# Norm scales spread over the partitions through a row in DRAM instead of by products with the identity

## The chip, the core and the metric

The program runs on one core of one Trainium2 chip. The metric is the device time of one execution in microseconds (us), the median over several. The core's engines work side by side, each through its own queue in order: TensorE (PE) multiplies matrices into PSUM, VectorE (DVE) and ScalarE (ACT) work on tiles, GpSimd (POOL) here does small powers, and SyncE (SP) issues the transfers (DMAs). Semaphores let one engine wait for another.

## The reference

Two layers of a decoder trunk over 512 tokens of width 1024, in float32. Per layer:

```
hn   = rms_norm(h, g_mix);  proj = hn @ w_in          # q | k | v | xr | gr
o    = rms_norm(diff_attention(rope(q), rope(k), v), g_subln) * (1 - lam_init)   # 4 heads
y    = rg_lru(conv(xr)) * gelu(gr)
h    = h + concat(o, y) @ w_out
h    = h + square(relu(rms_norm(h, g_mlp) @ w_mlp_in)) @ w_mlp_out
gate = sigmoid(rms_norm(h, g_ple) @ w_ple_gate)
h    = h + gate * (p[l] @ w_ple_proj)                 # the PLE step
out  = rms_norm(h, g_final)                           # after the last layer
```

Each rms_norm multiplies every token by one number, 1 / sqrt(mean square + eps).

## The kernel before

Activations lie transposed: a tile h[m] holds 128 features on the partitions and the 512 tokens along the free dimension. A product is done in three passes over split operands (high and low parts in a rounded float32 format), which `mm3` issues; a projection of 128 outputs is 8 x 3 = 24 products `dense` of 128x512. Weights come in chunks of 128x1024 (`raw`), and ACT and DVE split each into `wh` and `wl`.

A norm isn't applied to the input of a projection but to its output, since one number per token commutes with the product. `Norm.stats` sums squares over the partitions by four small products (`msq`) that leave the sums with the tokens on the partitions, 128x4; DVE adds eps (`me`), and POOL takes the power -0.5 (`rT`; for the MLP norm DVE takes the reciprocal, since the squared ReLU squares the factor, too). What multiplies a 128x512 output needs these 512 numbers along the free dimension and the same on all partitions. That is the job of `spread`. Before, it issues four products in which the identity is the moving operand and a column of r, broadcast to 128 columns, the stationary one. They are float32 and appear as two records each, eight per spread, under the name `bc`. For a norm ACT copies the result to SBUF (`rbc`); for a head of attention DVE multiplies from PSUM.

There are seven spreads per layer: the first norm (users: the multiplies `xp` behind the recurrent branch's projections, and more later), one for each of the four heads in `head_out` (sums `osm`, scales `orT`, multiply `o<-o`, then split into `oh` and `ol` for the output projection), the MLP norm (users: `dn` behind the down projection) and the PLE norm (users: `gt` behind the gate projection). The final norm, `FinalNorm`, has its own products of the name `bc`, which the change leaves.

The order of the work isn't the order of the code. `Plan` records every operation, and `Plan.schedule` lists them by a model: each engine has a clock, each operation a cost, the oldest ready operation of the engine that is free first is issued, and tiles come from pools of fixed size. A DMA is modelled as 1.15 us, then its bytes at 355 GB/s in one line with all other DMAs, then 0.9 us. `Plan.add` finds what an operation depends on by its tiles. Every operation therefore appears on one line of the profile, L182, and is told apart by its tiles.

PSUM holds six banks for projections and scores (tag `pm`) and two for small results (`ps`), among them `bc`. In the PLE step `ple` takes two banks for the `pj` products and two for the gates per pair of outputs, so the second pair's gates need banks that the first pair gives back.

Of the kernel before, what the change touches and what calls it, by code (L numbers as in the profile page):

```python
# [11 lines left out]
F32 = mybir.dt.float32  # L12
F32R = mybir.dt.float32r
I32 = mybir.dt.int32
AF = mybir.ActivationFunctionType
ALU = mybir.AluOpType
AX = mybir.AxisListType

S = 512
NT = S // 128  # L20
# [45 lines left out]
class Plan:  # L66
# [73 lines left out]
    def add(self, eng, fn, method, args, kw):  # L140
        i = len(self.nodes)
        outs = [a for a in list(args[:1]) + [kw.get("out"), kw.get("accum_out")] if hasattr(a, "free_size")]
        ins = [a for a in list(args[1:]) + [v for k, v in kw.items() if k not in ("out", "accum_out")]
               if hasattr(a, "free_size")]
        deps, uses = set(), set()
        for aps, write in ((ins, False), (outs, True)):
            for a in aps:
                if a.space == bass.MemoryType.DRAM:
                    continue
                t = self.tiles.get(a.name)  # L150
                if t is None:
                    t = self.tiles[a.name] = {"w": [], "r": [], "n": 0, "first": i,
                                              "tag": self.tags[self.index[a.name]] if a.name in self.index else None}
                deps.update(t["w"])
                if write:
                    deps.update(t["r"])
                uses.add(a.name)
        for a in ins:
            if a.name in self.tiles:
                self.tiles[a.name]["r"].append(i)  # L160
        for a in outs:
            t = self.tiles.get(a.name)
            if t is not None:
                t["w"], t["r"] = ([i], []) if t["r"] or eng == "pe" else (t["w"] + [i], [])
        for u in uses:
            self.tiles[u]["n"] += 1
        deps.discard(i)
        size = 0
        if "dma" in method:
            size = kw["out"].nbytes if not callable(kw["out"].nbytes) else kw["out"].nbytes()  # L170
        func = kw.get("func")
        self.nodes.append(dict(eng=eng, fn=fn, args=args, kw=kw, deps=deps, uses=uses, cost=self.cost(eng, method, args, kw),
                               pri=i - self.boost, size=size, set=self.SETS.get(func, 0)))
        if eng == "pe":
            out = args[0]
            rows = (kw["lhsT"] if "lhsT" in kw else args[1]).partition_size()
            self.nodes[-1]["cols"] = out.free_size() * rows / 128 * (1 if kw.get("rhs", out).dtype == F32R else 4 if "rhs" in kw else 2)
# [223 lines left out]
def build(ctx: ExitStack, tc: tile.TileContext, given, x, p, pos, w, vec, lamqk, out):  # L401
    rnc = tc.nc
    nc = Plan(rnc, WIN, ('raw', 'wh', 'wl'), given)
    act = nc.scalar.activation
    ve = nc.vector
    mm = nc.tensor.matmul
# [5 lines left out]
    wsp = ctx.enter_context(tc.tile_pool(name="ws", bufs=1))  # L412
    psm = ctx.enter_context(tc.tile_pool(name="psm", bufs=1, space=bass.MemoryType.PSUM))
    pss = ctx.enter_context(tc.tile_pool(name="pss", bufs=1, space=bass.MemoryType.PSUM))

    def T(name, dt=F32, n=S):
        return nc.tile(tp, [128, n], dt, "t", TB, name)
# [4 lines left out]
    def PS(name):  # L422
        return nc.tile(pss, [128, S], F32, "ps", 2, name)
# [71 lines left out]
    def take(kind, l, *rest):  # L495
        i = cur[0]
        assert CHUNKS[i] == (kind, l, *rest), (CHUNKS[i], kind, l, rest)
        w_split(i)
        cur[0] += 1
        return w_t.pop(i)  # L500
# [5 lines left out]
    def split(src, hi, lo):  # L506

        act(out=hi, in_=src, func=AF.Copy)
        ve.tensor_tensor(out=lo, in0=src, in1=hi.bitcast(F32), op=ALU.subtract)
# [11 lines left out]
    ident = const.tile([128, 128], F32, name="ident")  # L521
# [146 lines left out]
    class Norm:  # L668
# [33 lines left out]

        def spread(self):
            self.bc = T("rbc")
            spread(self.rT, 0, self.bc)

    def spread(r, c, dst):
        ps = PS("bc")
        for j in range(NT):
            mm(ps[:, j * 128:(j + 1) * 128], lhsT=r[:, c + j:c + j + 1].to_broadcast([128, 128]), rhs=ident,  # L710
               start=True, stop=True)
        if dst is None:
            return ps
        act(out=dst, in_=ps, func=AF.Copy)

    class FinalNorm:

# [57 lines left out]
    def layer(l, h, nm, last):  # L775
# [107 lines left out]
        for j in range(NT):  # L883
            hi, lo = T("vh", F32R), T("vl", F32R)
            r = nm.rT[:, j:j + 1]
# [115 lines left out]

        def head_out(hd):
            o, r = ho.pop(hd)
            ps = spread(r, 0, None)
            ve.tensor_tensor(out=o, in0=o, in1=ps, op=ALU.mult)
            hi, lo = T("oh", F32R), T("ol", F32R)
            split(o, hi, lo)
            yo[hd] = (hi, lo)

        def push_head(hd, q, k):  # L1010
            for qi in range(NT):
                unit_scores(hd, qi, q, k)
                unit_max(hd, qi)
                unit_mix(hd, qi)
                unit_T(hd, qi)
            head_av(hd)
            head_norm(hd)
            head_out(hd)
# [55 lines left out]
        for g in (ORDER[0:3], ORDER[3:6], ORDER[6:8]):  # L1074
            ws = []
            for m in g:
                c = take("out", l, m)
# [15 lines left out]
        for q in range(NQ):  # L1093
# [57 lines left out]
            for i0 in range(0, KD, 2):  # L1151
                ws = []
                for m in ORDER[i0:i0 + 2]:
                    c = take("down", l, m, q)
# [111 lines left out]
def trunk(tc, x, p, pos, w, vec, lamqk, out):  # L1266
    import concourse.bacc as bacc
    nc = bacc.Bacc("TRN2", target_bir_lowering=False, num_devices=1)
    a = [nc.dram_tensor(f"a{i}", t.shape, t.dtype, kind="ExternalInput").ap() for i, t in enumerate((x, p, pos, w, vec, lamqk, out))]
    with tile.TileContext(nc) as t0:  # L1270
        plan = build(t0, None, *a)
    build(tc, plan, x, p, pos, w, vec, lamqk, out)
# [64 lines left out]
```

## Time and profile before

| | us |
|---|---|
| median of 3 runs | 1205.5 (1205.45 to 1206.63) |
| profiled execution, its time | 1205.26 |
| its span | 1203.1 |
| PE busy | 1185.9 (99%), 6784 matmuls |
| DVE busy | 946.3 (79%) |
| ACT busy | 665.8 (55%) |
| POOL busy | 21.6 (2%) |

The span runs from the first to the last instruction of the program; the time holds 2.2 us more. A busy time is the union of an engine's records; PE's records overlap, so that the distance from one start to the next tells what a product costs, and not its record's length. The chain of waits follows the work that ended last back through what released it. Stretches in the trace are named by microseconds from the span's start: layer 0 has its attention from about 40 to 172 us, its MLP up to 547, its PLE step up to 592; layer 1 follows in the same way, with attention up to 761 and the PLE step from 1132 on.

### The profile page before, as it was taken

What the parts mean: (1) busy time and instruction counts of PE and PEld (TensorE: products, weight loads), DVE (VectorE), ACT (ScalarE), POOL (GpSimd) and SP (SyncE); (2) the same over time, 40 slices, a digit from 0 to 9 for tenths busy, and PEclk for the clock granted to TensorE, in tenths of its full rate; (3) what the DMA queues carried; (4) which work ended last, traced back from release to release, by engine and by line L of the source; (5) the groups of instructions that cost most, each with busy time, mean ns of one, the idle gap of its engine ahead of it and who ended that gap; (6) DMA issues with size and microseconds to landing.
All of it is one profiled execution on the core that took longest, in us unless ns stands there. A gap on an engine that the chain in (4) does not pass through costs nothing.

```text
span 1203.1 us, 17586 instructions
## 1 busy us (share of the span) xinstructions
PE 1185.9 (99%) x6784; PEld 1040.7 (87%) x6784; DVE 946.3 (79%) x1704; ACT 665.8 (55%) x1084; POOL 21.6 (2%) x44
## 2 busy tenths in 40 slices
PE   8999999999999999999999999999999999999996
PEld 6877788988988989988888888899899898898896
DVE  8899989987787678575778999898786787776564
ACT  6878747743643535543458787476355254364352
POOL 1000010000000000000000000000000000000000
PEclk9999999999999999999999999999999999999998
DMA  6321132243323333332323202324332333342202
GB/s 238 105 71 51 38 123 88 89 141 103 108 92 100 107 97 114 106 106 88 94 71 103 83 2 77 116 89 133 95 106 89 105 106 105 93 127 97 88 1 71
DMA packets 34371, 114.70 MB, mean 95 GB/s; under 512 B 3952, under 2 KB 6000, under 8 KB 34288
## 3 DMA queue, kind: packets, MB, share of 16 engines
q1 hardware_dynamic: 34288, 113.59, 30.0%
q8 instruction: 53, 0.87, 0.3%
q14 instruction: 30, 0.25, 0.1%
HBM read 111.48 MB, written 2.10 MB: 94 GB/s over the span
## 4 chain that ended last, share of the span: by engine, by line
PE 88%; DVE 6%; ACT 3%; DMA 1%; issue 1%; POOL 0%; SPq 0%; POOLq 0%; DVEq 0%; ACTq 0%
PE dense L182 53%; PE up L182 27%; PE pv L182 2%; PE pj L182 2%; PE bc L182 1%; DVE pr L182 1%; PE av L182 1%; DVE qr L182 1%; PE sc L182 1%; ACT ky L182 1%; DVE wl L182 1%; DVE q L182 1%; PE msq L182 1%; ACT pr L182 1%; POOL orT L182 0%
## 5 line engine op out<-in xcount | busy, mean ns | idle before, releaser
L182 ACT ACTIVATE wh<-raw 128x1024 fp32r<-128x1024 f32 x204 | 214.3, 1057 | 280.1 <-PE dense L182 150.3
L182 DVE TENSOR_TENSOR wl<-raw,wh 128x1024 fp32r<-128x1024 f32 x204 | 248.0, 1220 | 22.2 <-ACT wh L182 21.8
L182 PE MATMUL dense<-ffh,wh 128*128 128x512 f32 x512 | 199.5, 390 | 0.0
L182 PE MATMUL dense<-ffh,wl 128*128 128x512 f32 x512 | 199.3, 389 | 0.0
L182 PE MATMUL dense<-ffl,wh 128*128 128x512 f32 x512 | 199.3, 389 | 0.0
L182 PE MATMUL dense<-hgh,wl 128*128 128x512 f32 (+1 forms) x400 | 150.5, 376 | 1.4 <-DVE wl L182 1.2
L182 PE MATMUL dense<-hgl,wh 128*128 128x512 f32 (+1 forms) x400 | 150.9, 377 | 0.0
L182 PE MATMUL dense<-hgh,wh 128*128 128x512 f32 (+1 forms) x400 | 150.5, 376 | 0.1
L182 PEld LDWEIGHTS dense<-ffh,wl 128*128 128x128 f32 x512 | 96.1, 188 | 20.2
L182 PEld LDWEIGHTS dense<-ffh,wh 128*128 128x128 f32 x512 | 96.2, 188 | 19.6
L182 PEld LDWEIGHTS dense<-ffl,wh 128*128 128x128 f32 x512 | 96.2, 188 | 19.5
L182 DVE TENSOR_TENSOR dn<-dense,rbc 128x512 f32<-128x512 f32 x64 | 44.2, 691 | 73.4 <-PE dense L182 72.5
L182 PE MATMUL up<-bh,wl 128*128 128x256 f32 x352 | 99.6, 283 | 0.0
L182 PE MATMUL up<-bl,wh 128*128 128x256 f32 x352 | 99.6, 283 | 0.0
L182 PE MATMUL up<-bh,wh 128*128 128x256 f32 x352 | 99.5, 283 | 0.0
L182 ACT ACTIVATE sh<-s 128x512 fp32r<-128x512 f32 x96 | 60.0, 628 | 70.9 <-DVE s L182 70.2
L182 PEld LDWEIGHTS dense<-hgh,wl 128*128 128x128 f32 x400 | 75.5, 189 | 13.6 <-DVE wl L182 1.9
L182 PEld LDWEIGHTS dense<-hgh,wh 128*128 128x128 f32 x400 | 75.5, 189 | 12.2 <-DVE q L182 0.4
L182 PEld LDWEIGHTS dense<-hgl,wh 128*128 128x128 f32 x400 | 75.5, 189 | 12.0
L182 PE MATMUL up<-bh,sl 128*128 128x256 f32 x288 | 81.5, 283 | 0.0
L182 PE MATMUL up<-bl,sh 128*128 128x256 f32 x288 | 81.5, 283 | 0.0
L182 PE MATMUL up<-bh,sh 128*128 128x256 f32 x288 | 81.3, 283 | 0.0
(235 smaller groups left out, 2549.6 us busy)
## 6 DMA issues: line engine op xcount, KB each, us to landing
raw<-w SPq DMA_DIRECT2D x204, 512.0 KB, 3.6
h<-x SPq DMA_DIRECT2D x8, 256.0 KB, 5.3
out<-fin SPq DMA_DIRECT2D x8, 256.0 KB, 2.2
w<-w SPq DMA_DIRECT2D x4, 256.0 KB, 4.3
pT<-p SPq DMA_DIRECT2D x4, 256.0 KB, 3.3
lq<-lamqk SPq DMA_DIRECT2D x1, 256.0 KB, 7.1
vt<-vec SPq DMA_DIRECT2D x1, 61.0 KB, 2.2
posi<-pos SPq DMA_DIRECT2D x1, 2.0 KB, 2.9
```

The source lines that it names most:

```text
L182: d["fn"](*d["args"], **d["kw"])
```

## The change

`spread` no longer multiplies. It takes a tile of 4x128 in DRAM, writes the 128x4 scales into it token by token, and reads it back to all 128 partitions at once, both through POOL's DMA queue. The result lies in SBUF in each case, so a head gets a tile `obc`, and the ACT copy for the norms goes. `Plan.add` now follows tiles in DRAM as well, so the read waits for the write.

```
-                if a.space == bass.MemoryType.DRAM:
+                if a.space == bass.MemoryType.DRAM and a.name not in self.index:
...
+    drp = ctx.enter_context(tc.tile_pool(name="dr", bufs=1, space=bass.MemoryType.DRAM))
...
-            spread(self.rT, 0, self.bc)
-
-    def spread(r, c, dst):
-        ps = PS("bc")
-        for j in range(NT):
-            mm(ps[:, j * 128:(j + 1) * 128], lhsT=r[:, c + j:c + j + 1].to_broadcast([128, 128]), rhs=ident,
-               start=True, stop=True)
-        if dst is None:
-            return ps
-        act(out=dst, in_=ps, func=AF.Copy)
+            spread(self.rT, self.bc)
+
+    def spread(r, dst):
+
+        row = nc.tile(drp, [NT, 128], F32, "row", 4, "row")
+        nc.gpsimd.dma_start(out=row.rearrange("j p -> p j"), in_=r, allow_slow_non_contiguous=True)
+        nc.gpsimd.dma_start(out=dst, in_=row.rearrange("j p -> (j p)").unsqueeze(0).to_broadcast([128, S]))
...
-            ps = spread(r, 0, None)
-            ve.tensor_tensor(out=o, in0=o, in1=ps, op=ALU.mult)
+            bc = T("obc")
+            spread(r, bc)
+            ve.tensor_tensor(out=o, in0=o, in1=bc, op=ALU.mult)
```

The planner makes a new order from this. On PE, in the PLE step of layer 0, behind the statistics and the last six products of the first two gates:

```order
 L182 MATMUL pj<-pTh,wh 128x512
 L182 MATMUL pj<-pTl,wh 128x512
-L182 MATMUL bc<-ident,rT 128x128 x4
 L182 MATMUL pj<-pTh,wl 128x512
 L182 MATMUL pj<-pTh,wh 128x512
```

The group bc is taken out, and nothing else moves there: the twelve pj products stand where they stood, and behind them the gates of the second pair.

On DVE, at the first head of layer 0, from the mean square `ome` of the head's output to the multiply of that output; before:

```order
L182 SCALAR_TENSOR_TENSOR ome<-ome,osm 128x4
L182 TENSOR_TENSOR wl<-raw,wh 128x1024
L182 TENSOR_TENSOR kl<-q_398,ky 64x512
L182 TENSOR_TENSOR at<-tr,at 128x128
L182 TENSOR_TENSOR kl<-q_398,ky 64x512
L182 RECIPROCAL s_358<-s_358 128x1
L182 TENSOR_SCALAR mx<-mx 128x2
L182 TENSOR_TENSOR o<-o,bc 128x512
```

And now on DVE the last of the rows ahead of the same multiply, with the first behind it:

```order
L182 TENSOR_TENSOR at<-tr,at 128x128
L182 ISA pr,mx<-sc,mask 128x512
L182 ISA mx 128x1
L182 RECIPROCAL s_361<-s_361 128x1
L182 TENSOR_TENSOR wl<-raw,wh 128x1024
L182 SCALAR_TENSOR_TENSOR s_361<-s_361,nlam,s_352 128x1
L182 RECIPROCAL s_368<-s_368 128x1
L182 TENSOR_SCALAR mx<-mx 128x2
L182 SCALAR_TENSOR_TENSOR pr<-pr,s_361 128x256
L182 TENSOR_TENSOR wl<-raw,wh 128x1024
L182 TENSOR_TENSOR o<-o,obc 128x512
L182 TENSOR_TENSOR at<-tr,at 128x2x128
```

Twenty instructions stand between the two now, where six stood: softmax work of later blocks of the same head and a second weight split have moved ahead of the multiply.

## Rows read from the trace of the kernel before

**Rows 1.** The page: engines' busy time, and the weight queue (packets, MB, share).
```profile
PE 1185.9 (99%) x6784; PEld 1040.7 (87%) x6784; DVE 946.3 (79%) x1704; ACT 665.8 (55%) x1084; POOL 21.6 (2%) x44
...
q1 hardware_dynamic: 34288, 113.59, 30.0%
```

**Rows 2.** The chain of waits in order of time: start, duration, what.
```profile
20.23 0.79 PE msq L182 x8
...
30.74 1.16 PE bc L182 x8
...
167.93 0.80 PE osm L182 x8
...
168.99 1.93 POOL orT L182
...
251.91 0.89 PE bc L182 x8
...
503.03 43.55 PE dense L182 x192
```

**Rows 3.** Windows of both attention stages: length, PE, PEld, DVE, ACT, POOL busy, PE clock, DMA.
```profile
40.00:172.00 132.00, 127.49 (x633) 103.84 (x632) 125.47 (x299) 101.56 (x192) 6.84 (x4) 1.00 0.22 69
616.00:761.00 145.00, 144.64 (x717) 120.72 (x716) 131.96 (x298) 107.30 (x197) 5.23 (x4) 1.00 0.24 77
```

**Rows 4.** Timeline at the PLE norm of layer 0: start, duration, engine, operation.
```profile
559.46 0.49 PE L182 MATMUL dense<-hgh,wh 128*128 128x512 f32 x1
...
559.88 1.01 POOL L182 TENSOR_TENSOR rT<-me,mhalf 128x4 f32<-128x4 f32 x1 [388.97 <-DVE me L182]
...
561.41 1.05 PE L182 MATMUL bc<-ident,rT 128*128 128x128 f32 x8
...
562.22 0.47 PE L182 MATMUL pj<-pTh,wl 128*128 128x512 f32 x1
...
563.63 1.28 DVE L182 TENSOR_TENSOR gt<-dense,rbc 128x512 f32<-128x512 f32 x2
...
564.60 0.40 PE L182 MATMUL dense<-hgh,wh 128*128 128x512 f32 x1
```

**Rows 5.** Who waited for whom: us in total, times, longest.
```profile
PEld bc L182 <- POOL orT L182: 2.3, 4, 0.7
```

**Rows 6.** Groups by form, 100 to 172 us: busy, mean ns, idle before.
```profile
L182 DVE TENSOR_TENSOR wl<-raw,wh 128x1024 fp32r<-128x1024 f32 x11 | 13.4, 1217 | 0.0
...
L182 DVE CUSTOM_DVE_ANT_0 pr<-sc,mask 128x512 f32<-128x512 f32 x6 | 4.1, 686 | 0.0
...
L182 DVE TENSOR_TENSOR o<-o,bc 128x512 f32<-128x512 f32 x3 | 2.1, 687 | 0.9 <-PE bc L182 0.9
...
L182 ACT ACTIVATE oh<-o 128x512 fp32r<-128x512 f32 x3 | 1.9, 627 | 0.9 <-DVE o L182 0.9
```

**Rows 7.** DMA issues: times, KB each, median us from issue to landing.
```profile
out<-fin SPq DMA_DIRECT2D x8, 256.0 KB, 2.2
...
pT<-p SPq DMA_DIRECT2D x4, 256.0 KB, 3.3
lq<-lamqk SPq DMA_DIRECT2D x1, 256.0 KB, 7.1
vt<-vec SPq DMA_DIRECT2D x1, 61.0 KB, 2.2
posi<-pos SPq DMA_DIRECT2D x1, 2.0 KB, 2.9
```

**Rows 8.** The heads' scales on POOL: ns min/median/max.
```profile
L182 POOL TENSOR_TENSOR orT<-ome,mhalf x8: 1006/1455/1989, 110.8 to 757.1; 128x4 f32<-128x4 f32 x8
```

**Rows 9.** Windows around PE's waits at the start and end, columns as in rows 3.
```profile
8.00:12.00 4.00, 3.57 (x9) 2.32 (x10) 3.59 (x6) 4.00 (x8) 0.00 (x0) 0.59 1.02 376
...
1192.00:1196.00 4.00, 1.65 (x7) 1.57 (x8) 0.80 (x3) 0.81 (x2) 0.69 (x1) 0.65 0.00 0
1196.00:1200.00 4.00, 1.01 (x4) 0.72 (x4) 2.48 (x4) 0.00 (x0) 0.00 (x0) 0.50 0.34 113
```

## The prediction

> **What bounds the kernel now.** First the page: TensorE (PE) is busy for 1185.9 of 1203.1 us [rows 1], so look at the chain of waits: it is PE from end to end outside the attention stages, and a product of the form dense takes 43.55 / 192 = 0.227 us [rows 2]. Then the windows of the two attention stages: VectorE (DVE) is busy for 125.47 of 132 us in layer 0 and for 131.96 of 145 us in layer 1 [rows 3]. So there PE and DVE are both nearly full, and time lost on either ends up in the span; elsewhere only PE counts. POOL and the DMA queues are nearly idle: q1 takes 30.0% of the DMA engines [rows 1].
>
> **What goes.** Fourteen spreads (per layer one for the first norm, four heads, the MLP norm, the PLE norm) lose four float32 products with the identity each, eight records on PE. In the chain such a group stands at 0.89 to 1.16 us [rows 2]; at the PLE norm the next product starts 0.81 us after it [rows 4]. I take 0.9: 14 x 0.9 = 12.6 us off PE, all of it on the path outside attention (ends 11.3 and 16.2 by 0.81 and 1.16). PE's own wait for POOL ahead of these products goes too, 2.3 us [rows 5]. The six copies of the product on ScalarE (ACT) go from an engine that is busy for 55% [rows 1]: nothing. The multiply of a head reads the scales from SBUF instead of PSUM, 0.69 us as before [rows 6]: nothing.
>
> **What comes.** Each spread becomes two DMAs on POOL's queue, the second behind the first's landing, and the multiply on DVE behind the second. POOL has only the next power behind them, and SP's queue of weight loads isn't passed. What counts is D, the time from r (the 128x4 scales) to the landed 128x512 tile. No transfer before is issued by POOL, goes out in 4-byte pieces, or goes through DRAM, so D is bounded from landings [rows 7]. Low: two of the shortest, vt and out, 2.2 + 2.2 = 4.4 us. High: the row is 512 pieces, 32 per engine; a packet took 0.300 x 16 x 1203.1 / 34288 = 0.168 us of an engine [rows 1], so 2.2 + 32 x 0.168 = 7.6; the read back has the shape of lq, 7.1 us beside the opening loads; together 14.7. Nearest rows: posi moves 128 pieces of 16 bytes in 2.9, 0.7 above vt; four times as many pieces, 2.2 + 4 x 0.7 = 5.0; pT brings 256 KB in 3.3. I take D = 5.0 + 3.3 = 8.3 us.
>
> The Trainium skill, "DMA: Bandwidth & Descriptors", section "Anatomy of one DMA — SWDGE (gpsimd) path", gives a POOL-issued DMA about 2.0 us plus its bytes at 436 GB/s, which would make D an estimated 4.6 us; the 2.2 us of out is the row here nearest to that, but from SP's queue. The same page, section "Rules for kernel authors", says that a strided last dimension becomes one descriptor per element and advises against it, which speaks against the row write; no run so far shows its price.
>
> **PLE norm, twice.** r is ready at 559.88 + 1.01 = 560.89, PE is past the statistics at 559.46 and has 6 + 12 products until it needs a PSUM bank that the first gate multiply gives back (the order shows the same 18 with bc taken out): 559.46 + 18 x 0.227 = 563.5. The bank is free at 560.89 + 8.3 + 0.7 = 569.9. PE waits 6.4 us; before it went on without a wait [rows 4]. Behind that multiply on DVE stand the second gate and all of h. Two layers: 12.8 us.
>
> **Heads 0 to 2 of each layer.** The planner has put DVE work under its guess of the transfers: in the new order 20 instructions stand between ome and o of the first head, before 6. By the durations of their forms (two weight splits wl at 1.22, two masked maxima pr at 0.69, and 16 shorter ones of 0.69 down to 0.08; [rows 6] has the first two) they sum to 8.3 us. The power takes 1.0 to 2.0 us [rows 8], 1.7 with its handoffs, and D follows: DVE waits 1.7 + 8.3 - 8.3 = 1.7 us; the other heads have 7.4 to 8.5 us of such work, so I take 2.0. Behind o on DVE stand pr and at, for which the transposes wait, and DVE has 5% to 9% of slack. Six heads: 12 us.
>
> **Last head of each layer.** 45 products follow its osm before the output projection needs oh. PE is there at 168.73 + 45 x 0.227 = 178.9. Oh is there at 170.92 + 8.3 + 0.69 + 0.63 = 180.5 [rows 2, 6]. 1.6 us; in layer 1, with a power of 1.0, 0.7. Together 2.3.
>
> **Layer starts.** In layer 0 r comes at 30.7, where bc started. PE passes msq at 21.0 and has 73 products, until 37.6, before the third V group needs the bank of the first xr group, free at 30.7 + 8.3 + 0.8 = 39.8 [rows 2]: 2.2 us. In layer 1 there are 63 products, then the gates of the recurrence, which need three multiplies and a convolution first: nothing to 1 us, I take 0.7.
>
> **MLP norm, twice.** r is made in the up projection, and the first product that depends on the spread stands 133 and 155 instructions later, some 30 us of PE. Nothing, even at D = 14.7.
>
> **Clock.** Behind the last gates, where PE was busy for 1.65 of 4 us, the granted clock fell to 0.65 and then 0.50, which is 1.2 GHz; after the opening waits it was 0.59 over 4 us [rows 9]. Two waits of 6.4 us should do this too: 4 x 0.41 = 1.6 us each, 3.3.
>
> **Sum.** -12.6 - 2.3 + 12.8 + 12 + 2.3 + 2.9 + 3.3 = +18.4 us. The profiled execution took 1205.26 us, 2.2 above its span and within 0.3 of the median 1205.5: 1205.3 + 18.4 = 1223.7, say **1224 us**. Around it each us of D counts at 12 places. At the low end, D = 4.4, only PLE still waits, 2 x 2.5: 1205.3 - 14.9 + 5.0 = 1195.4. At 14.7: 1224 + 6.4 x 12 = 1301.
>
> **Rivals.**
> A, the transfers land like the shortest rows. With D of 4.4 to 6 the DVE work covers them and only PLE waits, 5.0 to 8.2 us against 14.9 gained: 1195 to 1199 us, faster. For it: out, a write to DRAM, lands in 2.2. Against: that is from SP in long pieces, and posi's short ones were slower. The page's 2.0 us and bytes would give this case, an estimated 1196. The sides change at about D = 6.8, where PLE costs 2 x 4.9, the heads about 3 and the clock 2 to 3.
>
> B, the 4-byte pieces go one after another. With D of 11 or more all twelve waits are longer by at least 2.7: 1256 us and up, slower. For it: a packet's mean 0.168 us. Against: those are mostly 4 KB packets, and a small one should be shorter. The page's rule of one descriptor per element points here.
>
> C, the removal is hidden anyway in attention. Eight of the 14 groups stand in stretches where DVE is busy for 95% and 91% [rows 3], so their 7.2 us come off an engine that would wait for DVE: 1231 us, slower. For it: those shares. Against: PE too is busy for 127.5 of 132 and 144.6 of 145 there.
>
> **How the numbers follow.** The forecast (D of 7 to 10, 1208 to 1244 us) gets 0.42, A 0.27, B 0.18, C 0.13. Under 0.2% (2.4 us) this kernel's time can't be told from no change; A's upper edge (0.02) and the forecast's lower one (0.05) make 0.07 the same, the rest of A 0.25 faster, and 0.37 + 0.18 + 0.13 = 0.68 slower. The range of 1196 to 1262 leaves out A's lowest part (0.05) and most of B (0.13). The forecast's own range is 1208 to 1244.
>
> **What would show it.** In the profile of the changed kernel: row and rbc landings that sum to 7 to 10 us from r; at PLE, DVE gt waiting on a DMA and PE standing still for 5 to 8 us, twice, with a granted clock under 1 behind it; DVE o waiting on a DMA about 2 us in six heads; no wait at dn; PE's products of bc down to those of the final norm. It is wrong if the two landings sum to under 6.8 us (then faster), if PE's idle time is not at these places, or if time is lost in the MLP stages, where I expect none.

## The result, and the profile after

The changed kernel takes 1337.1 us (1333.0 to 1337.7, median of 4 runs) where the kernel before takes 1206.1 on the same chip: 1.108 times as long, with an interval of 1.106 to 1.110, or 131 us more. The prediction said 1224, in a range of 1196 to 1262: the direction was right, the size was not.

The page of the changed kernel's profile, against [rows 1]:

```profile
span 1335.0 us, 17406 instructions
...
PE 1209.6 (91%) x6672; PEld 1051.4 (79%) x6672; DVE 947.2 (71%) x1704; ACT 664.3 (50%) x1078; POOL 38.5 (3%) x72
```

The work is nearly the same. PE has lost 112 records, 14 groups of 8; its share of the span fell from 99% to 91%. So the 132 us are waiting, and products at a lower clock. The DMA issues of the changed kernel, where the last column is the median time from issue to landing, against [rows 7]:

```profile
raw<-w SPq DMA_DIRECT2D x204, 512.0 KB, 3.6
...
obc<-row POOLq DMA_DIRECT2D x8, 256.0 KB, 4.1
...
rbc<-row POOLq DMA_DIRECT2D x6, 256.0 KB, 4.5
...
row<-orT POOLq DMA_DIRECT2D x8, 2.0 KB, 9.3
row<-rT POOLq DMA_DIRECT2D x6, 2.0 KB, 9.5
```

Writing 2 KB takes over twice as long as reading 256 KB back. With 0.3 us from the power to the write's issue and 0.6 from its landing to the issue of the read, D, the time from the scales to the landed tile, is 0.3 + 9.3 + 0.6 + 4.1 = 14.3 us for a head and 0.3 + 9.5 + 0.6 + 4.5 = 14.9 for a norm; the prediction took 8.3. The timeline of the changed kernel at the PLE norm of layer 0, against [rows 4] (start, duration, engine, operation, in brackets the idle time before it and what ended that):

```profile
611.70 1.04 POOL L182 TENSOR_TENSOR rT<-me,mhalf 128x4 f32<-128x4 f32 x1 [292.75 <-DVE me L182]
...
613.03 0.81 POOL L182 DMA_DIRECT2D row<-rT  x1 [0.29 <-POOL rT L182]
...
615.27 0.39 PE L182 MATMUL pj<-pTh,wl 128*128 128x512 f32 x1
...
623.10 0.56 POOL L182 DMA_DIRECT2D rbc<-row  x1 [9.26 <-DMA row<-rT]
629.77 1.29 DVE L182 TENSOR_TENSOR gt<-dense,rbc 128x512 f32<-128x512 f32 x2 [11.98 <-DMA rbc<-row]
...
630.51 0.79 PE L182 MATMUL dense<-hgh,wh 128*128 128x512 f32 x1 [14.85 <-DVE gt L182]
...
631.10 0.63 PE L182 MATMUL dense<-hgl,wh 128*128 128x512 f32 x1
```

PE issues the last pj product at 615.27 and the next gate at 630.51: it stands still for 15.0 us beyond one product. Here D runs from the end of the power, 611.70 + 1.04 = 612.74, to the start of the multiply: 629.77 - 612.74 = 17.0 us, the longest of the fourteen. The place and the chain (row, read, multiply, PSUM bank, PE) are those of the prediction.

The windows of this stretch (length, PE, PEld, DVE, ACT, POOL busy, granted clock, DMA share, GB/s), against [rows 9]:

```profile
612.00:616.00 4.00, 3.66 (x16) 2.65 (x15) 2.36 (x2) 2.54 (x3) 1.54 (x2) 1.00 1.08 28
616.00:620.00 4.00, 0.00 (x0) 0.00 (x0) 1.23 (x1) 0.53 (x1) 0.00 (x0) 0.89 0.51 25
620.00:624.00 4.00, 0.00 (x0) 0.00 (x0) 0.00 (x0) 0.00 (x0) 0.56 (x1) 0.50 0.76 27
624.00:628.00 4.00, 0.00 (x0) 0.00 (x0) 0.00 (x0) 0.00 (x0) 0.00 (x0) 0.50 0.85 334
...
632.00:636.00 4.00, 4.00 (x11) 3.12 (x10) 3.43 (x6) 2.38 (x4) 0.00 (x0) 0.50 0.02 4
636.00:640.00 4.00, 4.00 (x18) 3.24 (x18) 1.18 (x3) 1.26 (x2) 0.00 (x0) 0.97 0.00 0
```

Two things are to be seen. Behind the wait the granted clock is 0.50, which is 1.2 GHz, for some 6 us of work: 11 products in 4 us where 18 fit. Behind the layer starts, the eight heads and the PLE norm of layer 1 the windows show 0.50, too. And from 612 to 624 the DMA engines are 0.5 to 1.1 busy while they move 25 to 28 GB/s; then a like share moves 334. So they are held for most of this time by something other than data. Three weight chunks are under way in these 28 us, and in the issues of this window alone they land much later than the 3.6 us of the whole run:

```profile
raw<-w SPq DMA_DIRECT2D x3, 512.0 KB, 11.6
rbc<-row POOLq DMA_DIRECT2D x1, 256.0 KB, 6.6
```

The row's own packets take at most 0.2 us each. It is packets of the weight queue that stay open: in the whole trace 137 of them take over 2 us each, 133 of these while a row write is under way; before, none does. The read back here, issued behind them, takes 6.6 us, too.

The attention stages of the changed kernel, against [rows 3], are at about 40 to 187 and 640 to 800 us:

```profile
40.00:187.00 147.00, 119.12 (x518) 96.25 (x519) 110.07 (x262) 95.40 (x169) 6.57 (x8) 0.87 0.20 49
640.00:800.00 160.00, 144.22 (x646) 117.62 (x645) 116.80 (x222) 91.48 (x150) 5.18 (x6) 0.95 0.25 70
```

PE, busy for 97% and 100% before, is now busy for 81% and 90%. Who waits for whom (us in total, times, longest):

```profile
DVE o L182 <- DMA obc<-row: 65.1, 8, 9.6
...
DVE s L182 <- DMA raw<-w: 31.9, 7, 12.2
...
PEld dense L182 <- DVE gt L182: 27.0, 2, 15.3
...
ACT wh L182 <- DMA raw<-w: 16.6, 9, 4.5
```

The first row is the wait of the heads, the third that of the PLE norms. The second is DVE, which sums up weight chunks (`s`) and waits for them longest behind the MLP norms' rows (12.2 us), where PE doesn't stand still; ACT's waits for weights have not grown (20.1 us in the kernel before).

The bill is read from PE's starts: from one to the next a product should take what products of its form usually take, 0.227 us for `dense`. Distances that exceed this by over 0.55 us sum to 120.1 us of excess (9.7 before). The smaller excesses sum to 47.8 (15.9 before; these two sums hang on the distance taken as usual, by 1 to 2 us), and what they grew by lies almost wholly in stretches at half the clock. That is +110.4 and +31.9, less 12.6 for the products of bc, a figure of the prediction: +129.7 of the 131.9 by which the span grew.

### The profile page after: what moved, and what is told of

It is laid out like the page before. It is cut to its first block, busy times and chain, and to the rows that moved or that the text cites. A ratio compares the mean times of both kernels' runs of the same rounds, so it can differ in the third digit from the quotient of the medians.

```text
span 1335.0 us, 17406 instructions
## 1 busy us (share of the span) xinstructions
PE 1209.6 (91%) x6672; PEld 1051.4 (79%) x6672; DVE 947.2 (71%) x1704; ACT 664.3 (50%) x1078; POOL 38.5 (3%) x72
## 5 line engine op out<-in xcount | busy, mean ns | idle before, releaser
L182 PE MATMUL dense<-hgh,wh 128*128 128x512 f32 (+1 forms) x400 | 157.1, 393 | 26.3 <-DVE gt L182 26.1
L182 PE MATMUL dense<-hgh,wl 128*128 128x512 f32 (+1 forms) x400 | 157.6, 394 | 4.1 <-DVE wl L182 4.1
L182 PE MATMUL dense<-hgl,wh 128*128 128x512 f32 (+1 forms) x400 | 155.4, 388 | 0.0
L182 PEld LDWEIGHTS dense<-hgh,wh 128*128 128x128 f32 x400 | 79.1, 198 | 40.4 <-DVE gt L182 27.0
L182 PEld LDWEIGHTS dense<-hgh,wl 128*128 128x128 f32 x400 | 79.2, 198 | 18.2 <-DVE wl L182 5.0
L182 PEld LDWEIGHTS dense<-hgl,wh 128*128 128x128 f32 x400 | 79.1, 198 | 13.3
```

Of the source, the lines that this page charges most:

```text
L182: d["fn"](*d["args"], **d["kw"])
```

## The experiments

Each ran beside the kernel before on the same chip (1205.6 to 1206.4 us, and 1204.1 for the last one). The row's landing is a median; where two numbers stand, the first is that of the heads and the second that of the norms. The times of e1, e2, e8, e9, e11, e5, e6 and e13 are single executions, and those of the changed kernel lie up to 4.7 us apart, so differences of a few microseconds between them tell nothing.

| run | edit | row lands | time |
|---|---|---|---|
| e1_sp | row written from SP's queue | 8.9, 10.3 | 1332.6 |
| e2_p16 | 128 pieces of 16 bytes | 1.9, 3.0 | 1231.0 |
| e3_tr | transposed on PE, 4 pieces of 512 bytes | 3.0 | 1235.5 |
| e8_adj | 512 pieces, each beside its partition's others | 8.7 | 1332.7 |
| e9_cols | four writes of 128 pieces | 8.5, 9.4 | 1318.3 |
| e11_one | one write of 128 pieces | 8.4, 8.7 | 1385.6 |
| e4_told | planner told of the ways' length | 9.2, 9.3 | 1287.0 |
| e10_fill | products in the PLE waits | 10.1, 10.6 | 1338.3 |
| e5_norms | norms alone through DRAM | 10.3 | 1264.9 |
| e6_heads | heads alone through DRAM | 9.9 | 1286.7 |
| e7_mlp | MLP norms alone | 11.2 | 1204.1 |
| e12_mlptr | MLP norms alone, transposed | 4.4 | 1203.7 |
| e13_forms | seven forms beside the kernel before | 1.6 to 10.7 | 1219.3 |

### Is it the queue or the pieces?

```
-        nc.gpsimd.dma_start(out=row.rearrange("j p -> p j"), in_=r, ...)
+        nc.sync.dma_start(out=row.rearrange("j p -> p j"), in_=r, ...)
```

> The row write is issued by SyncE's queue instead of POOL's; its 512 pieces of 4 bytes and all else stay. Theory P (pieces: DRAM takes long to confirm 512 scattered 4-byte writes; the data packets were out 1.75 us after the issue and the landing came at 9.3): the write still lands 8 to 10 us after its issue, and the time stays between 1310 and 1370 us. Rival Q (POOL's software queue is slow whatever it carries): the write lands like SyncE's other short transfers, 2.2 to 3.1 us, the way from scales to tile falls by some 6 us at 12 places, and the time to 1225 to 1265 us.

In its DMA issues:

```profile
row<-orT SPq DMA_DIRECT2D x8, 2.0 KB, 8.9
row<-rT SPq DMA_DIRECT2D x6, 2.0 KB, 10.3
```

From SP's queue the write lands no earlier, and the time is about that of the changed kernel: it is not POOL's queue. Next the same 2 KB in 128 pieces:

```
-        row = nc.tile(drp, [NT, 128], F32, "row", 4, "row")
-        nc.gpsimd.dma_start(out=row.rearrange("j p -> p j"), in_=r, ...)
+        row = nc.tile(drp, [128, NT], F32, "row", 4, "row")
+        nc.gpsimd.dma_start(out=row, in_=r)
```

> The row lies in DRAM as 128x4, so the write has 128 pieces of 16 bytes instead of 512 of 4, and the read takes it as it lies (the scales reach the wrong tokens: the permutation is left out). P, by the piece: of the 9.3 us some 7.6 scale with the pieces, landing 1.75 + 7.6 / 4 = 3.7 us, 5.6 us less at 12 places: 1260 to 1280 us. Q: the landing stays at 8 to 10 us and the time at 1325 to 1350.

Its DMA issues (times, KB each, median us from issue to landing):

```profile
obc<-row POOLq DMA_DIRECT2D x8, 256.0 KB, 3.5
...
rbc<-row POOLq DMA_DIRECT2D x6, 256.0 KB, 4.4
...
row<-orT POOLq DMA_DIRECT2D x8, 2.0 KB, 1.9
row<-rT POOLq DMA_DIRECT2D x6, 2.0 KB, 3.0
```

The write lands in 1.9 and 3.0 us (medians) and 106 of the 131 us are gone; no weight packet takes over 2 us. So it is the pieces; the gain is larger than theory P gave (1260 to 1280 us, from a landing of 3.7). The scales can also be kept in order: PE transposes them to 4x128, DVE copies them out of PSUM, and 4 rows of 512 bytes are written.

```
+        ps = PS("rt")
+        nc.tensor.transpose(ps[0:NT, 0:128], r, ident)
+        rt = SM("rt", 128)
+        ve.tensor_copy(out=rt[0:NT, :], in_=ps[0:NT, 0:128])
+        nc.gpsimd.dma_start(out=row, in_=rt[0:NT, :])
```

> TensorE first transposes the 128x4 scales to 4x128 (one product with the identity instead of four), VectorE copies them to SBUF, and POOL writes 4 pieces of 512 bytes. P: the write lands in 2.0 to 2.7 us; with 0.6 us for transpose and copy the way is 9.3 - 2.4 - 0.6 = 6 us shorter at 12 places: 1235 to 1270 us. Q: the landing stays above 8 us and the time is 1335 to 1360 us.

It took 1.024 times the time before (interval 1.021 to 1.027); the row lands in 3.0 us, the read in 3.7 to 4.0, and PE still waits 8.4 and 5.9 us at the PLE norms. So even with short landings the change loses.

### Which property of the pieces?

Of e8_adj, the four scales of a partition lie beside each other in DRAM, but reach the DMA as four pieces (a copy spaces them in SBUF):

```
+        r2 = SM("r2", 2 * NT).rearrange("p (j t) -> p j t", t=2)[:, :, 0]
+        ve.tensor_copy(out=r2, in_=r)
+        nc.gpsimd.dma_start(out=row, in_=r2, ...)
```

> The row lies in DRAM as 128x4 as in e2_p16, but VectorE first copies the scales to every second column of a small tile, so the write again has 512 pieces of 4 bytes, which now lie next to each other in DRAM (tokens in the wrong order: the permutation is left out). Theory F (the number of 4-byte pieces is what DRAM takes long to confirm): landing at 8 to 10 us and 1320 to 1345 us. Theory S (it is the scatter: each piece 512 bytes from the next, so no two go out together): landing at 2 to 3 us and 1230 to 1245 us, as e2_p16.

The row lands in 8.7 us and the time is 1332.7: in this order, too, 4-byte pieces are slow, and theory S falls. Of e9_cols, four writes of one column each:

```
+        for j in range(NT):
+            nc.gpsimd.dma_start(out=row[j:j + 1, :].rearrange("j p -> p j"), in_=r[:, j:j + 1], ...)
```

> Four row writes per spread, one per column of the scales: each has 128 pieces of 4 bytes that lie next to each other in DRAM; the same 512 pieces in all, the right order. S: each lands in 2 to 3 us, the last some 2 us later for three more issues: 1240 to 1265 us. F: landings of 8 us or more, 1320 to 1350 us. If it is the number of pieces in one transfer alone, a quarter each: 1.75 + 7.6 / 4 = 3.7 us, and some 1265 us.

The writes land in 8.5 us (heads) and 9.4 us (norms) at the median, single ones in 7.3 to 17.2, the longest the last of the four at a PLE norm; the total is just under the 1320 that theory F gave. Then one column alone, a quarter of the pieces:

```
+        nc.gpsimd.dma_start(out=row.rearrange("j p -> p j"), in_=r[:, 0:1], ...)
+        nc.gpsimd.dma_start(out=dst.rearrange("q (j p) -> q j p", p=128),
+                            in_=row.unsqueeze(0).to_broadcast([128, NT, 128]))
```

> The full change, but only the first of the four columns of scales is written, 128 pieces of 4 bytes instead of 512, and the read repeats it four times; so the scales of tokens 128 to 511 are left out. Theory NUMBER (the landing goes with the number of pieces): row lands in 2 to 3.5 us, like the 128 pieces of 16 bytes, no weight packet takes over 2 us, total 1225 to 1240 us. Rival SIZE (a piece of 4 bytes is slow by its size, however few there are): row lands over 5 us, total over 1265 us.

The DMA issues of this kernel:

```profile
obc<-row POOLq DMA_DIRECT2D x8, 256.0 KB, 9.4
...
rbc<-row POOLq DMA_DIRECT2D x6, 256.0 KB, 9.5
...
row<-orT POOLq DMA_DIRECT2D x8, 0.5 KB, 8.4
row<-rT POOLq DMA_DIRECT2D x6, 0.5 KB, 8.7
```

The theory NUMBER falls: 128 pieces take nearly as long as 512. The total goes far beyond both theories because this read, which takes the same 512 bytes four times for each partition, lands in 9.4 us instead of 4.1; why was not separated. It does test the count of sites: D is 0.3 + 8.4 + 0.6 + 9.4 = 18.7 for a head, 4.4 more than in the changed kernel, 12 x 4.4 = 53, and 1337 + 53 = 1390 against 1385.6 measured.

Whether it is the size of a piece or its place was settled by adding seven forms of the write to the kernel before. All its spreads stay products, and nothing waits for the writes:

```
+            bc = products(r)
+            probe(r)      # one dma_start of r, or part of it, to DRAM; form by site
...
+            o, i = to([128, 16], "g4x128")[:, 0:1], r[:, 0:1]     # 128 pieces, 64 bytes apart
+            o, i = to([128, NT, 16], "g4x512")[:, :, 0], r        # 512 pieces, 64 bytes apart
```

> The kernel before, all spreads by products, and at each of the 14 spreads one write of the scales (or a part of them) to DRAM on POOL's queue that nothing waits for, in seven forms, each once per layer: 512, 128 and 16 pieces of 4 bytes that lie next to each other in DRAM, 256 of 8 bytes, 128 of 16 bytes, and 128 and 512 pieces of 4 bytes that lie 64 bytes apart in DRAM. Theory SIZE (a piece of 4 bytes is slow by its size): the five 4-byte forms land at 8 to 13 us whatever their number and place, those of 8 and 16 bytes at 2 to 4. Rival NEIGHBOURS (small pieces that share the same stretch of DRAM hold each other up): the two spaced forms land at 2 to 4 us as well. Rival NUMBER (refuted for 128 unless that run's reads confused it): 16 pieces land at 2, 128 at 3, 512 at 9. The total stays within 1204 to 1209 us in each case, since nothing waits for these writes.

In its DMA issues, p4x is a form of 4-byte neighbours (2.0 KB: 512 pieces, 0.5: 128, 0.1: 16), p8x and p16x have 8 and 16 bytes, g4x 4 bytes at 64 bytes' distance; the KB of g4x are those of the data.

```profile
p4x<-orT POOLq DMA_DIRECT2D x2, 0.5 KB, 8.8
...
p4x<-rT POOLq DMA_DIRECT2D x1, 2.0 KB, 9.7
p4x<-orT POOLq DMA_DIRECT2D x1, 0.1 KB, 1.6
p8x<-orT POOLq DMA_DIRECT2D x1, 2.0 KB, 4.8
p16x<-orT POOLq DMA_DIRECT2D x1, 2.0 KB, 2.8
g4x<-rT POOLq DMA_DIRECT2D x1, 0.5 KB, 3.8
g4x<-rT POOLq DMA_DIRECT2D x1, 2.0 KB, 3.0
p16x<-rT POOLq DMA_DIRECT2D x1, 2.0 KB, 1.9
g4x<-orT POOLq DMA_DIRECT2D x1, 0.5 KB, 1.8
g4x<-orT POOLq DMA_DIRECT2D x1, 2.0 KB, 2.2
p4x<-orT POOLq DMA_DIRECT2D x1, 2.0 KB, 10.7
p4x<-rT POOLq DMA_DIRECT2D x1, 0.1 KB, 4.0
p8x<-rT POOLq DMA_DIRECT2D x1, 2.0 KB, 3.5
```

NEIGHBOURS is right: 512 pieces of 4 bytes land in 2.2 and 3.0 us when they lie 64 bytes apart, and in 9.7 and 10.7 when they touch. Touching pieces of 8 bytes lie between (3.5 and 4.8), and touching ones of 16 bytes are quick (1.9 and 2.8). Only 16 touching pieces of 4 bytes land in 1.6 and 4.0, so it takes more than a few; what holds between 16 and 128 pieces, or at distances between 4 and 64 bytes, stays open, and so does what happens in DRAM.

The total, expected within 1209, was 1219.3. Most of the reason is in its trace. A write of 128 touching pieces is issued at 114.58; the windows behind that, with the columns as above:

```profile
116.00:120.00 4.00, 3.67 (x19) 3.10 (x19) 4.00 (x10) 3.75 (x10) 0.00 (x0) 1.00 0.45 16
120.00:124.00 4.00, 4.00 (x21) 3.25 (x21) 3.88 (x11) 0.21 (x2) 0.00 (x0) 1.00 0.43 26
124.00:128.00 4.00, 1.80 (x10) 1.19 (x8) 0.00 (x0) 0.08 (x1) 0.00 (x0) 1.00 0.65 189
```

and the wait between 110 and 130 us:

```profile
ACT wh L182 <- DMA raw<-w: 7.7, 1, 7.7
```

The DMA engines are held at 16 to 26 GB/s, weights come late, and ACT stands at the split wh, DVE behind ACT and PE behind both, although nobody waits for the write itself. PE loses 5.2 us here and 5.8 at the head of layer 1 where 512 touching pieces are written, and behind both the granted clock is 0.50. At the two other sites with 128 or 512 touching pieces PE doesn't wait. So such pieces can cost twice: by their own landing, and by what they hold up.

### Which sites, and what else is in the bill?

The planner's model of a transfer was given the measured lengths (first kernel), and 48 useless products were put behind the PLE statistics so that PE stays busy there (second):

```
                 end = dma + 0.9
+                if e == "pool":
+                    end = s + (10.0 if d["size"] <= 2048 else 5.2)
```

```
             nm3.spread()
+            for _ in range(48):
+                mm(ps, lhsT=z[:, 0:128], rhs=z, start=True, stop=True)
```

> The transfers stay; the planner is told that POOL's row write ends 10.0 us and its read 5.2 us after the issue, as the trace has them, instead of some 2.1 and 2.8. Theory O (the order was made for a way of 5 us, and another order hides 15): the waits in the heads and at the layer starts go (about 80 of 105 us, and their share of the lowered clock), those at PLE stay (26 us): 1225 to 1265 us. Rival N (there is no independent work to put there: six PSUM banks, 600 operations of window): above 1300 us.

> The changed kernel, with 48 useless products of 0.227 us (10.9 us) on TensorE behind the statistics of each PLE norm, where TensorE stood for 15.0 and 11.4 us. Theory K (the waits cost twice, since TensorE ran at half its clock for some 5.7 us after each of them): 2.85 us per place come back, 5 to 6 us less than the changed kernel's 1337: 1331 us. Rival (the wait is all, the low clock falls where nothing is behind it): within 1.5 us of 1337.

The time of e4_told lies between its theories: 1287.0, ratio 1.067 (1.063 to 1.072). PE's waits fall from 120 to 78 us; the PLE norms keep 14.7 and 11.2, as theory O expected, the layer starts lose theirs, and the first three heads of each layer keep 3 to 6 each. So a planner that knows the lengths buys back 50 of the 131 us, not the whole loss.

e10_fill is a miss. At the PLE norm its timeline shows PE at work through most of the wait:

```profile
618.33 11.19 PE L182 MATMUL fill<-hgh 128*128 128x512 f32 x48
...
620.09 0.81 POOL L182 DMA_DIRECT2D row<-rT  x1 [0.29 <-POOL rT L182]
...
634.58 1.29 DVE L182 TENSOR_TENSOR gt<-dense,rbc 128x512 f32<-128x512 f32 x2 [15.91 <-DMA rbc<-row]
```

The 48 products take 11.2 us, no half clock stands behind them, and the excess of slow products falls from 47.8 to 39.4 us. But the time is 1338.3 (1336.5 to 1340.2), not below the changed kernel's 1337.1. In this profile the rows land 0.8 to 1.1 us later, and the heads and layer starts wait some 12 us longer in all. e5_norms and e6_heads, which ran on the same chip as e10_fill and keep the write as it is, land late as well (10.3 and 9.9), so a difference between chips isn't excluded. What took the gain back wasn't settled; that the clock's share would come back in full if PE were kept busy is therefore not shown.

The change was then split by sites (products kept at the others):

> The six norms go through DRAM as in the change, the eight heads by products as before. Site by site from the changed kernel's trace: waits at the norms 9.6 + 15.0 + 9.3 + 11.4 = 45 us, half clock behind the four 11 us, six groups of products gone -5: 1257 us. Rival (the waits share slack, so that one part alone costs clearly less than its share, or more): under 1245 or over 1270 us.

> Only the eight heads' spreads go through DRAM; the six norms keep their products. The run with the norms alone through DRAM took 1264.9 us, 59 above before, and the full change is 131 above. Theory ADD (each site costs what it waits and the clock behind it, one site independent of the next): 131 - 59 = 72 above before, about 1278 us, window 1268 to 1290; row landings of 8 to 10.5 us at eight heads, waits of PE of 5 to 10 us at each, none at the PLE norms. Rival COVER (with the products of the norms back, the planner has more to put under the heads' ways): under 1260 us.

The norms alone cost 58.6 us (1264.9, between the forecast of 1257 and the rival's 1270), the heads alone 81.1 (1286.7): together 139.6 against 131, so the sites add up nearly as ADD says; COVER falls. Last, the only sites where no wait was predicted or seen, in two forms:

> Only the two MLP norms' spreads go through DRAM, by the same 512 pieces of 4 bytes; all others keep their products. Theory HIDDEN (the prediction's: some 30 us of products lie between r and its first user): row and read land 13 to 16 us behind r, PE waits nowhere for them, and eight float32 records go from PE twice, 2 x 0.9 us: 1204.3 us, window 1203 to 1205.5, the granted clock 1.00 there. Rival JAM (the weight transfers that stand behind the 4-byte pieces in the DMA engines reach PE, since the up projection needs a new chunk every few us): PE waits for weights behind the two sites, and the time is 1206 to 1212.

> As the run with the MLP norms alone through DRAM, but PE transposes the 128x4 scales first and DVE copies them, so that the write is 4 pieces of 512 bytes. Theory HIDDEN: row lands in 1.6 to 3 us and the read in 3.5 to 4.5, nothing waits; eight records go and one small transpose comes, twice: about 1204.6 us, window 1203.3 to 1206. Rival JAM: if the 4-byte pieces' jam costs the other kernel PE time, this one is faster than it by over 1.5 us.

They take 0.9985 (0.9976 to 0.9994) and 0.9982 (0.9973 to 0.9991) of the time before, over 11 executions each: 1.5 and 1.9 us less than the kernel before, a small gain, but clear of the noise. HIDDEN is right on the time and the waits in both: PE waits nowhere for these transfers. Three of the ways were longer than it said: row and read together took 17.7 and 13.5 us in e7_mlp (13 to 16 expected), and the rows of e12_mlptr landed in 4.6 and 4.2 (1.6 to 3). The intervals overlap; that the touching pieces cost anything in the up projection isn't shown, though 32 weight packets take over 2 us in e7_mlp and none in e12_mlptr.

## Why the prediction was wrong, point by point

- **What goes.** Right: 112 records fewer, and two groups by themselves gave 1.5 us (0.7 to 2.9) against the 1.8 charged. A slip of 2 us: the 2.3 us of [rows 5] are waits of the weight loads; PE itself waited 0.6 us for `orT`. Rival C, that removal inside attention is worth nothing, was not separated; it is a matter of 7 us.
- **D, the failed step: "four times as many pieces, 2.2 + 4 x 0.7 = 5.0".** The write lands in 9.3 to 9.5 us, above even the bound of 7.6. The working took the price of a piece from posi, a read whose 16-byte pieces spread to 128 partitions, and scaled it by number. The runs show that the price isn't in the number (128 pieces take 8.4 to 8.8) but in small pieces that touch in DRAM; with pieces of 16 bytes 106 of the 131 us go. No row of before holds such a write, so the bound should have been open upward rather than closed by a mean packet's time. The read back was put at 3.3 and took 4.1 to 4.5, up to 6.6 behind held-up weights.
- **The slope, 12 places.** Right. PE's waits at the places, measured: PLE 15.0 + 11.4 us (12.8 predicted for both), six heads 47.8 (12), last heads 12.0 (2.3), layer starts 19.0 (2.9), MLP norms none (none). That is 105 of the 110 us by which the waits grew. The prediction's 30.0 with 6.4 us more at each of the 12 places, for D = 14.7, would be 107, and its sum 1301 us. At a head, the predicted wait of DVE, 1.7 us at D = 8.3, becomes 7.7 at the measured 14.3; the 65.1 us in 8 waits above are 8.1 each.
- **Clock, the second mis-sized term.** 3.3 us predicted, for the PLE norms only; 31.9 measured. The term took 1.6 us for each of two waits, from [rows 9], and put the other ten places at nothing without a reason; the trace shows half the clock behind all twelve. Over them it is 31.9 / 12 = 2.7 each; why more than 1.6 was not separated. 1301 + 31.9 - 3.3 = 1330, against 1337 measured.
- **Held-up weights.** Put at nothing: "SP's queue of weight loads isn't passed" looked at the order in the queue, and not at the DMA engines, which both queues use. e13_forms shows 11 us of PE's waits from this alone, at two of its sites. In the changed kernel the share isn't separated: there it shows in longer reads.
- **Rivals.** B had the right time, 1256 us and up, with a chance of 0.18, and the range cut most of it off. It blamed the 4-byte pieces, rightly; but its reason, that they go out one after another, doesn't hold: 128 take nearly as long as 512, and 512 that don't touch take 2.2 to 3.0 us. A would have needed a D under 6.8. e2_p16 has 0.3 + 1.9 + 0.6 + 3.5 = 6.3 for a head and 8.3 for a norm, which by the prediction's working leaves waits only at the PLE norms and layer starts and gives some 1210 us; it took 1231. Its trace has some 30 us more of waits and 8.5 more of slow products than before. So even with short ways the sum is some 20 us too low, and A's point of change probably too high; how much of that is the new order's own was not separated.

The Trainium skill, "DMA: Bandwidth & Descriptors", section "Anatomy of one DMA — SWDGE (gpsimd) path", puts a POOL-issued DMA at about 2.0 us plus its bytes. The spaced and the 16-byte forms of e13_forms come near that (1.8 to 3.8 us); the row of the changed kernel, 9.3 us, lies some 7 us above it, and the measurement decides. The same section of the Trainium skill says that most of the fixed time is the wait for the target memory's receipt of the last byte. The trace of the changed kernel fits that, but doesn't show the receipt: at eight of the fourteen rows the records of the data packets end within 1.8 us of the issue, and the landing comes at 8.0 to 9.8.

## What to carry to other kernels

A short dependent way through DRAM is priced by its landing, and that landing must come from a row of the same form: piece size, and what lies beside it in DRAM. Where none exists, leave the upper bound open. Each microsecond of such a way counts once per site that no work covers, and the lower clock behind a wait of PE is to be charged at every one of them. Put such a way only where tens of microseconds of other work lie in front of its user, and write whole rows.

## What the runs showed of the hardware that was not expected

- Small pieces of a write that touch in DRAM: 512 pieces of 4 bytes, written alone, landed in 7.5 to 13.5 us, 256 of 8 bytes in 3.5 to 4.8, 128 of 16 bytes in 1.7 to 4.6, and 512 of 4 bytes at 64 bytes' distance in 2.2 to 3.0.
- Between the issue of such a write and its landing, the same DMA engines hardly serve the other queue: 0.43 to 0.76 busy at 16 to 27 GB/s, and weight chunks issued in that time land mostly in 7.5 to 14 us instead of 3.6.
- The queue that issues the write makes little difference (medians of 8.9 and 10.3 us from SP, 9.3 and 9.5 from POOL).
- A read of 256 KB to 128 partitions that takes one and the same 512 bytes four times for each took 9.4 us (median), against 4.1 from a row of 2 KB.
